# One value product for both parts of the attention weights, with changed scratch rings and later requests

## The chip, the cores and the metric

The kernel runs on one core of a Trainium2 chip. The metric is the device time of one execution in microseconds. Engines are named as in the profile: PE is TensorE, DVE VectorE, ACT ScalarE, POOL GpSimd, and SP the SyncE queue, from which most transfers are issued.

## What is computed

One layer of a bidirectional encoder on 1024 tokens (16 rows of 64) of width 1024, in float32. The reference, cut to the part in which the change lies:

```
h = h + 0.5 * swiglu(rms_norm(h, ffn1_norm), ...)
u = rms_norm(h, mix_norm);  z = u @ w_in
q, k, v, s_in, gates = split(z)
y_attn = neighbourhood_attention(q, k, v, na_rpb) @ w_attn_out   # 8 heads of 64, window 8 x 16
y_ssm  = s5_branch(s_in, ...) @ w_ssm_out                        # two scans, GELU, GLU
h = h + (sigmoid(g_attn) * y_attn + sigmoid(g_ssm) * y_ssm) @ w_out
h = h + 0.5 * swiglu(rms_norm(h, ffn2_norm), ...)
h = h + (p @ w_ple) * sigmoid(rms_norm(h, ple_norm) @ w_ple_gate)
out = rms_norm(h, final_norm)
```

In the attention, scores = q k / 8 + bias inside the window, a softmax, and the sum over the values v.

## The kernel before

**Precision in two parts.** The activations lie transposed, features on partitions and tokens along the free dimension, mostly as tiles of 128x512. A float32 operand is split into a high part (an ACT cast to fp32r) and a low part (a DVE subtraction); `split`, lines 152 to 154. A product is then three matmuls, high by high, high by low, low by high; `mm3`, lines 182 to 186.

**The order.** The order of TensorE's instructions is the program's (`manual_schedule` for PE, line 1801). For the other engines and the queues a planner with a time simulation orders them at build time (line 1800), except where a `manual_schedule` names DVE and ACT as well, as around `end()` (line 1723). Attention, scans and the GLU are written as a generator, `mixer_side` (line 1291). Projections call `tick()` after each three matmuls; when the count of a `yield n` has run down, the generator issues its next piece. So the attention units stand between pieces of the projections of q, k and the gates.

**Attention.** A unit is one head (8), one half of the rows (`rb`, 2) and one block of 16 columns (`cb`, 4): 64 units of 128 queries. Unit j issues `attn_scores` for itself (two matmuls; a DVE operation that adds the bias and finds the maximum; exponential, reciprocal and scaling), then `attn_turn` for unit j - 3, then `attn_values` for unit j - 5.

- `attn_turn` (line 1224) transposes three blocks of weights into one PSUM bank and splits them into `pth` (ACT) and `ptl` (DVE), two hid tiles of 128x384.
- `attn_values` (line 1235) does six matmuls. The values of a head lie side by side as high and low part, 64 columns each (`vhl`). With both as weights and `pth` as moving operand (128 columns), rows 0 to 63 of the bank O get high times high, rows 64 to 127 low times high (line 1240). With the high part alone as weights and `ptl` as moving operand, high times low is added to rows 0 to 63 (line 1242). One bank holds the four column blocks of a head half. After the fourth, ACT copies rows 64 to 127 out (line 1246), DVE adds the rest (line 1247), and the sum goes to `o_d`.
- `load_v` (line 1168) fetches values with four DMAs on SP into `vf` and splits them; `load_bias` (line 1181) fetches the bias rows of a head half into the single buffer `bt`, asked for in `make_tabs` right after the former ones were used.

From unit 48 on, `ssm_out` is added to each unit: two `emi` tiles are loaded by SP, and three units later six matmuls into the bank `yo` follow, whose copy goes to `y_d`. Lines 1356 to 1361 run the GLU after the last unit.

**Rings.** All 8 PSUM banks are one ring. In SBUF the tag `x` has 56 slots of 128x512: 32 for `u` (two halves, 8 tiles, high and low), the rest for hid tiles (`vhl`, the scores `sm`, `pth`, `ptl`, `emi`, the GLU's `yh`, `yl`, `wgh`, `wgl`) and later the operands of the branch products. In the middle stage the scratch kind `tmp` has a ring of its own with 4 buffers (line 1040): `vf`, `row`, `ot`, `ol`, `ys`, `gs`, `vs`, `sg`, `wgs`, `xn` and others. The kind `st`, for 128x1024 loads, has 3.

**Around it.** `gate_tile` (line 1365) computes one gate tile, copies it out of PSUM with ACT and stores it from SP to `g_d` at once. `load_br` (line 1405) loads the attention output of one half of the tokens from `o_d` for the branch products `br` (line 1490), two tiles of 128x1024, and splits them. `rstd` (line 204) is the reciprocal root of the norms: one ACT operation and three of DVE; `Norm.stat` (line 244) calls it. `end` (line 1683) writes out the order of the last steps.

Of the kernel before, what the change touches and what calls it, by code (L numbers as in the profile page):

```python
# [38 lines left out]
def encoder_block(ctx, tc, I, out):  # L39
# [50 lines left out]
    def dtile(name, shape):  # L90
        return dr.tile(list(shape), F32, name=name)
# [21 lines left out]
    a2_d = dtile("a2_d", [NF // 2, 7, P, HT])  # L113
    h2_d = dtile("h2_d", [P, NK * SEQ])
    v_d = dtile("v_d", [SEQ, 512])
    o_d = dtile("o_d", [512, SEQ])
    g_d = dtile("g_d", [16, P, SEQ])
    y_d = dtile("y_d", [NPD, P, NCH])
    y2_d = dtile("y2_d", [512, SEQ])
# [36 lines left out]
    def ksl(k):  # L156
        return slice(k * P, (k + 1) * P)
# [43 lines left out]

        return tc.issue_after(mark["ins"]) if "ins" in mark else nullcontext()

    def rstd(m, r, q):
        A.activation(r, m, AF.Abs_reciprocal_sqrt, bias=eps)
        V.tensor_tensor(q, r, r, ALU.mult)
        V.scalar_tensor_tensor(q, m, eps, q, ALU.add, ALU.mult)
        V.scalar_tensor_tensor(r, q, -3.0, r, ALU.add, ALU.mult)

    class Norm:  # L210
# [33 lines left out]
        def stat(self, r=None, summed=False):  # L244
            if summed:
                m = self.acc
            else:
                m = bank("ms")[:, 0:self.n]
                sums = [self.acc] + self.more
                for i, sq in enumerate(sums):  # L250
                    T.matmul(m, lhsT=ones, rhs=sq, start=i == 0, stop=i == len(sums) - 1)
            q = tmq("rq", [P, self.n])
            r = thid("rs", [P, self.n], F32) if r is None else r
            rstd(m, r, q)
            self.r = r

        def apply(self, gi, res, every):
# [779 lines left out]
    win = I["win"]  # L1037
    ap_cm = tc.tile_pool(name="ap", bufs=1, reuse_waits="tile")
    ap_ = ap_cm.__enter__()
    cur.update(st=(ap_, "st", 3), w=(ap_, "w", 12), tmp=(ap_, "tmp", 4))  # L1040

    def proj(w, t, name):
        o = bank(name)
# [123 lines left out]

    def load_v(hd, cb):
        n = 4 * KNC[cb]
        vf = tmp("vf", [P, 4, 64])  # L1170
        for g in range(4):
            nc.sync.dma_start(vf[0:n, g],
                              vdr[4 * g:4 * g + 4, KC0[cb]:KC0[cb] + KNC[cb], hd * 64:(hd + 1) * 64])
# [14 lines left out]
    def make_tabs(hd, rb):  # L1188
        b = 2 * hd + rb
        row = tmp("row", [P, 12, 32])  # L1190
        V.tensor_tensor(row, bts.pop(b),
                        rowm[:, rb].unsqueeze(2).broadcast_to([P, 12, 32]), ALU.add)
        load_bias(b + 1)
        res = []
        for v in range(3):
            n, f0 = (24, 32, 24)[v], (8, 0, 0)[v]
            tb = ap_.tile([P, 12, 32], F32, tag="tb", bufs=3, name="tb")
            V.tensor_tensor(tb[:, :, 0:n], row[:, :, f0:f0 + n],
                            colm[:, v, f0:f0 + n].unsqueeze(1).broadcast_to([P, 12, n]), ALU.add)
            res.append(tb)  # L1200
        tabs[hd, rb] = res
# [22 lines left out]
    def attn_turn(cb, sm):  # L1224
        kp = 4 * KNC[cb]
        tp = bank("pt")
        for g in range(3):
            T.transpose(tp[0:kp, ksl(g)], sm[:, g * kp:(g + 1) * kp], ident)
        ph = thid("pth", [P, 384])
        pl = thid("ptl", [P, 384])  # L1230
        A.copy(ph[0:kp], tp[0:kp, 0:384])
        V.tensor_tensor(pl[0:kp], tp[0:kp, 0:384], ph[0:kp].bitcast(F32), ALU.subtract)
        return ph, pl

    def attn_values(hd, rb, cb, O, ph, pl):
        kp = 4 * KNC[cb]
        hl = vld[hd, cb]
        for g in range(3):

            T.matmul(O[:, ksl(cb)], lhsT=hl[0:kp, rb + g].rearrange("p h d -> p (h d)"), rhs=ph[0:kp, ksl(g)], start=(g == 0), stop=False,  # L1240
                     skip_group_check=True)
            T.matmul(O[0:64, ksl(cb)], lhsT=hl[0:kp, rb + g, 0], rhs=pl[0:kp, ksl(g)], start=False, stop=(g == 2),
                     skip_group_check=True)
        if cb == 3:
            ot, ol = tmp("ot"), tmp("ol")
            A.copy(ol[0:64], O[64:128])
            V.tensor_tensor(ot[0:64].rearrange("p (r b c) -> p b r c", r=8, b=4),
                            O[0:64].rearrange("p (b r c) -> p b r c", b=4, r=8),
                            ol[0:64].rearrange("p (b r c) -> p b r c", b=4, r=8), ALU.add)
            nc.scalar.dma_start(o_d[hd * 64:(hd + 1) * 64, hsl(rb)], ot[0:64])  # L1250


    ydr = y_d.rearrange("g (t o) c -> g o t c", o=16)
# [37 lines left out]
    def mixer_side():  # L1291
        yield from u_second(14, 1)
        yield 8
        for r in range(2):
            V.memset(Xv[:, r, :, 0:1], 0.0)
            V.memset(Xv[:, r, :, XP - 1:XP], 0.0)
        ld = {}
        for pr in range(NPAIR):
            if pr in (0, 8):
                while pr // 4 not in stored:  # L1300
                    yield 1
                yield 8
                ld[pr] = inject_load(pr)
                yield 8
            if pr % 8 < 7:
                ld[pr + 1] = inject_load(pr + 1)
            inject(pr, *ld.pop(pr))
            yield 3
        while 0 not in qkv:
            scan_steps(1)  # L1310
            yield 1
        units = [(hd, rb, cb) for hd in range(NH) for rb in range(2) for cb in range(4)]
        n = len(units)
        for cb in range(4):
            load_v(0, cb)
        load_bias(0)
        make_tabs(0, 0)
        scan_steps(4)
        yield 6
        sms, pts, O = {}, {}, {}  # L1320
        so = {}
        SO = 48
        for j in range(n + 6):
            if j < n:
                hd, rb, cb = units[j]
                while hd not in qkv:
                    yield 1
                if cb == 0 and j > 0:
                    make_tabs(hd, rb)
                sms[j] = attn_scores(hd, rb, cb)  # L1330
            if 0 <= j - 3 < n:
                pts[j - 3] = attn_turn(units[j - 3][2], sms.pop(j - 3))
            if 0 <= j - 5 < n:
                hd, rb, cb = units[j - 5]
                if cb == 0:
                    O[hd, rb] = bank("O")
                attn_values(hd, rb, cb, O[hd, rb], *pts.pop(j - 5))
                if rb == 1 and hd + 1 < NH:
                    load_v(hd + 1, cb)
# [12 lines left out]
        yield 4  # L1352
        for m in range(4):
            glu_load(m)
        yield 13
        for t in range(2):
            glu_split(t)
            yield 4
            for m in range(4):
                glu_out(m, t)  # L1360
                yield 4

    start(mixer_side())

    def gate_tile(w, m, t):
        o = proj(w, t, "gt")
        gs = tmp("gs")
        A.copy(gs, o)
        nc.sync.dma_start(g_d[m, :, hsl(t)], gs)


    for m0 in range(0, 4, 2):
# [32 lines left out]
    def load_br(t, b):  # L1405

        res = []
        if b == 0:
            for k in range(0, 4, 2):
                st = tst("br")  # L1410
                nc.sync.dma_start(st.rearrange("p (k c) -> p k c", k=2),
                                  o_d[k * P:(k + 2) * P, hsl(t)].rearrange("(k p) c -> p k c", p=P))
                for i in range(2):
                    hi, lo = tx("bh"), tx("bl")
                    split(hi, lo, st[:, hsl(i)])
                    res.append((hi, lo))
            return res
        for k in range(4):
# [33 lines left out]
    W = [loadw(win[16 + m]) for m in (14, 15)]  # L1452
    for i in range(2):
        gate_tile(W[i], 14 + i, 0)
    drain()
    oy = [[load_br(0, 0)], []]
    W0 = [load_was(0)]
# [1 line left out]
    oy[0].append(load_br(0, 1))  # L1459
    for i in range(2):  # L1460
        gate_tile(W[i], 14 + i, 1)
    for b in range(2):
        oy[1].append(load_br(1, b))

# [218 lines left out]
    def end():  # L1683
# [131 lines left out]
```

## Time and profile before

| | |
|---|---|
| three runs | 2103.85, 2105.74, 2106.14 us; median 2105.74 |
| profiled execution: its time, its span | 2107.16 us, 2105.4 us |
| granted clock of TensorE, mean | 0.998 |
| HBM read, written | 201.01 MB, 82.31 MB |
| attention units | first scores at 838.5 us, last values at 1108.9 us |
| copies to `o_d`, and the branch products' first matmul | last at 1113.8 us; 1172.3 us |

How to read the rows: a group shows line, engine, operation, out<-in by the program's names, the shapes, the count, and then busy time, mean duration and the engine's idle time ahead of it with what ended it. A wait row shows who waited for whom, and then the total in us, the number of waits and the longest. A timeline row has its start in us from the span's start, its duration and, in brackets, the idle time before it. A tile row shows the shortest, median and longest duration in ns, first and last start, and the forms. A window row shows the length and then busy time and instruction count of PE, PEld (weight loads), DVE, ACT and POOL, the granted clock, the DMA engines' busy share and GB/s. Matmuls overlap: the next one starts while the one before it still drains, so the distance from start to start tells what one costs, not its duration.

### The profile page before, as it was taken

How to read it: one execution, taken by the hardware profiler on the slowest of the kernel's cores; microseconds unless marked ns; L12 is line 12 of the kernel's file. 1: busy time of each engine (PE TensorE's matmuls, PEld its weight loads, DVE VectorE, ACT ScalarE, POOL GpSimd, SP SyncE). 2: the span in 40 equal slices, each digit the busy share in tenths (PEclk: the TensorE clock that was granted, in tenths of full speed). 3: DMA queues.
4: the chain of work that ended last, by engine and by line, in shares of the span. 5: the costliest groups of instructions: out<-in, count | busy, mean ns of one | idle time of the engine just before them, and what ended most of it. 6: DMA issues, size and time to landing. Idle time of an engine off the chain costs nothing.

```text
span 2105.4 us, 28053 instructions
## 1 busy us (share of the span) xinstructions
PE 2078.4 (99%) x9662; PEld 1706.3 (81%) x9662; DVE 1417.4 (67%) x2420; ACT 1000.4 (48%) x1832; POOL 399.9 (19%) x636
## 2 busy tenths in 40 slices
PE   8999999999999999999999999899999999999998
PEld 3788888888888888888888888688888888888886
DVE  7897776667967334677653668886566665786855
ACT  6434333434445333666774635543333334445543
POOL 0037555541000006888200011000000000000000
PEclk9999999999999999999999999999999999999999
DMA  3435344475543552233467754143323238533302
GB/s 133 143 118 153 126 135 126 140 267 167 185 120 106 168 176 68 64 97 98 126 201 261 255 171 93 53 157 112 110 85 126 90 113 295 159 109 91 120 21 81
DMA packets 197744, 285.19 MB, mean 135 GB/s; under 512 B 41568, under 2 KB 81120, under 8 KB 197600
## 3 DMA queue, kind: packets, MB, share of 16 engines
q1 hardware_dynamic: 180304, 258.20, 38.9%
q10 hardware_dynamic: 14992, 21.00, 2.9%
q0 software_dynamic: 2304, 4.20, 1.3%
q8 instruction: 76, 1.25, 0.2%
q14 instruction: 68, 0.56, 0.1%
HBM read 201.01 MB, written 82.31 MB: 135 GB/s over the span
## 4 chain that ended last, share of the span: by engine, by line
PE 91%; DVE 4%; DMA 2%; ACT 2%; issue 1%; SPq 0%; DVEq 0%; ACTq 0%
PE dx L184 4%; PE dx L186 4%; PE dx L185 4%; PE ux L184 3%; PE ux L185 3%; PE gx L184 3%; PE ux L186 3%; PE gx L185 3%; PE gx L186 3%; PE gt L184 3%; PE gt L185 3%; PE gt L186 3%; PE dy L184 2%; PE dy L185 2%; PE dy L186 2%; PE uy L184 2%
## 5 line engine op out<-in xcount | busy, mean ns | idle before, releaser
L153 ACT CAST wh<-hbuf 128x512 fp32r<-128x512 f32 x280 | 172.9, 622 | 389.8 <-PE gx L185 80.9
L154 DVE TENSOR_TENSOR wl<-hbuf,wh 128x512 fp32r<-128x512 f32 x280 | 210.7, 755 | 124.6 <-ACT wh L153 122.3
L153 ACT CAST wh<-wblk 128x512 fp32r<-128x512 f32 x190 | 117.9, 622 | 187.0 <-PE dx L185 80.6
L184 PE MATMUL dx<-ah,wh 128*128 128x512 f32 x416 | 164.4, 395 | 3.2 <-DVE hbuf L1559 2.9
L154 DVE TENSOR_TENSOR wl<-wblk,wh 128x512 fp32r<-128x512 f32 x190 | 130.3, 689 | 52.7 <-ACT wh L153 47.3
L186 PE MATMUL dx<-ah,wl 128*128 128x512 f32 x416 | 162.6, 391 | 0.0
L185 PE MATMUL dx<-al,wh 128*128 128x512 f32 x416 | 162.4, 390 | 0.0
L154 DVE TENSOR_TENSOR al<-araw,ah 128x512 fp32r<-128x512 f32 x154 | 106.0, 692 | 51.9 <-PE dx L185 21.1
L1097 POOL TENSOR_TENSOR sc<-X,rho 128x128 f32<-128x128 f32 x128 | 76.8, 600 | 329.0 <-ACT X L1080 319.1
L184 PE MATMUL gx<-xh,wh 128*128 128x512 f32 x320 | 125.1, 391 | 1.2 <-DVE c L580 1.2
L184 PE MATMUL ux<-xh,wh 128*128 128x512 f32 x320 | 125.1, 391 | 0.4 <-DVE c L580 0.4
L186 PE MATMUL gx<-xh,wl 128*128 128x512 f32 x320 | 124.5, 389 | 0.0
L186 PE MATMUL ux<-xh,wl 128*128 128x512 f32 x320 | 124.5, 389 | 0.0
L185 PE MATMUL gx<-xl,wh 128*128 128x512 f32 x320 | 124.5, 389 | 0.0
L185 PE MATMUL ux<-xl,wh 128*128 128x512 f32 x320 | 124.5, 389 | 0.0
L153 ACT CAST ah<-araw 128x512 fp32r<-128x512 f32 x154 | 95.0, 619 | 46.0 <-PE dx L185 12.7
L184 PE MATMUL gt<-xh,wh 128*128 128x512 f32 x256 | 102.7, 401 | 0.0
L186 PE MATMUL gt<-xh,wl 128*128 128x512 f32 x256 | 99.8, 390 | 0.0
L185 PE MATMUL gt<-xl,wh 128*128 128x512 f32 x256 | 99.8, 390 | 0.0
L184 PEld LDWEIGHTS dx<-ah,wh 128*128 128x128 f32 x416 | 78.5, 189 | 22.0 <-DVE hbuf L1559 3.9
L185 PEld LDWEIGHTS dx<-al,wh 128*128 128x128 f32 x416 | 78.5, 189 | 16.8 <-issue 0.7
L186 PEld LDWEIGHTS dx<-ah,wl 128*128 128x128 f32 x416 | 78.4, 189 | 16.6
(381 smaller groups left out, 5605.2 us busy)
## 6 DMA issues: line engine op xcount, KB each, us to landing
araw<-a_d SPq DMA_DIRECT2D x154, 256.0 KB
a_d<-c SPq DMA_DIRECT2D x148, 256.0 KB
wblk<-in_wd SPq DMA_DIRECT2D x88, 256.0 KB
hbuf<-in_wg SPq DMA_DIRECT2D x40, 512.0 KB
hbuf<-in_wu SPq DMA_DIRECT2D x40, 512.0 KB
wst<-in_win SPq DMA_DIRECT2D x26, 512.0 KB
hbuf<-in_xT SPq DMA_DIRECT2D x32, 256.0 KB
h_d<-hbuf ACTq DMA_DIRECT2D x32, 256.0 KB
```

Source lines behind the costliest of these rows:

```text
L153: A.copy(hi, src)
L154: return eng.tensor_tensor(lo, src, hi.bitcast(F32), ALU.subtract)
L184: T.matmul(o, lhsT=wh, rhs=xh, start=first, stop=False, skip_group_check=more)
L185: T.matmul(o, lhsT=wh, rhs=xl, start=False, stop=False, skip_group_check=more)
L186: T.matmul(o, lhsT=wl, rhs=xh, start=False, stop=last, skip_group_check=more)
L1097: G.tensor_tensor(sc, both, rho4, ALU.mult)
```

## The change

- `attn_turn` writes both parts of the transposed weights into one tile `ptb` (three blocks, each with 128 high and 128 low columns) in a ring of two in the middle stage's pool; `attn_values` does one product of 256 columns for each block. A bank O holds two column blocks, with the products of the high and of the low weights beside each other.
- After each second block, ACT copies rows 64 to 127 (low values by high weights) and rows 0 to 63 (high by high) of the bank's high columns, and DVE adds rows 0 to 63 of its low columns. The two sums are stored as two planes of `o_d`; `load_br` loads both planes and adds them with DVE. Low values by low weights are computed too and not used.
- In a unit, `attn_values` (and `load_v`) is issued ahead of `attn_turn`.
- The kind `tmp` of the middle stage is taken from the ring `x`; `vf` has two buffers of its own.
- The bias rows are asked for at the third column block of a head half, in place of directly after the use of the former ones.
- A gate's store is issued after the copy of the next gate tile; `store_gate()` without arguments issues the one that is held.
- `rstd` and `stat` take a function `mid`, called after the ACT operation; in `end` the scalings of the tiles 6 and 7 move there.

```
-    o_d = dtile("o_d", [512, SEQ])
+    o_d = dtile("o_d", [2, 512, SEQ])
...
-    def rstd(m, r, q):
+    def rstd(m, r, q, mid=None):
         A.activation(r, m, AF.Abs_reciprocal_sqrt, bias=eps)
+        if mid is not None:
+            mid()
         V.tensor_tensor(q, r, r, ALU.mult)
...
-    cur.update(st=(ap_, "st", 3), w=(ap_, "w", 12), tmp=(ap_, "tmp", 4))
+    cur.update(st=(ap_, "st", 3), w=(ap_, "w", 12), tmp=(sb, "x", NX))
...
-        vf = tmp("vf", [P, 4, 64])
+        vf = ap_.tile([P, 4, 64], F32, tag="vf", bufs=2, name="vf")
...
                         rowm[:, rb].unsqueeze(2).broadcast_to([P, 12, 32]), ALU.add)
-        load_bias(b + 1)
...
-        ph = thid("pth", [P, 384])
-        pl = thid("ptl", [P, 384])
-        A.copy(ph[0:kp], tp[0:kp, 0:384])
-        V.tensor_tensor(pl[0:kp], tp[0:kp, 0:384], ph[0:kp].bitcast(F32), ALU.subtract)
-        return ph, pl
+        pb = ap_.tile([P, 3, 2, P], F32R, tag="ptb", bufs=2, name="ptb")
+        src = tp[0:kp, 0:384].rearrange("p (g q) -> p g q", g=3)
+        A.copy(pb[0:kp, :, 0], src)
+        V.tensor_tensor(pb[0:kp, :, 1], src, pb[0:kp, :, 0].bitcast(F32), ALU.subtract)
+        return pb
...
+        o = O["o"][:, (cb % 2) * 256:(cb % 2) * 256 + 256]
         for g in range(3):
-            T.matmul(O[:, ksl(cb)], lhsT=hl[0:kp, rb + g].rearrange("p h d -> p (h d)"), rhs=ph[0:kp, ksl(g)], start=(g == 0), stop=False,
+            T.matmul(o, lhsT=hl[0:kp, rb + g].rearrange("p h d -> p (h d)"), rhs=pb[0:kp, g].rearrange("p h q -> p (h q)"), start=(g == 0), stop=(g == 2),
                      skip_group_check=True)
-            T.matmul(O[0:64, ksl(cb)], lhsT=hl[0:kp, rb + g, 0], rhs=pl[0:kp, ksl(g)], start=False, stop=(g == 2),
-                     skip_group_check=True)
+        if cb % 2 == 0:
+            return
+        if cb == 1:
+            O["t"] = tmp("ot")
+        ov = O["t"].rearrange("p (r b c) -> p b r c", r=8, b=4)[:, cb - 1:cb + 1]
+        src = O["o"].rearrange("p (b h r c) -> p h b r c", b=2, h=2, r=8)
+        A.copy(ov[64:128], src[64:128, 0])
+        A.copy(ov[0:64], src[0:64, 0])
+        V.tensor_tensor(ov[0:64], src[0:64, 1], ov[0:64], ALU.add)
         if cb == 3:
...
-            nc.scalar.dma_start(o_d[hd * 64:(hd + 1) * 64, hsl(rb)], ot[0:64])
+            nc.scalar.dma_start(o_d[:, hd * 64:(hd + 1) * 64, hsl(rb)], O["t"])
...
+                if cb == 2:
+                    load_bias(2 * hd + rb + 1)
                 sms[j] = attn_scores(hd, rb, cb)
+            if 0 <= j - 5 < n:
+                hd, rb, cb = units[j - 5]
+                if cb % 2 == 0:
+                    O.setdefault((hd, rb), {})["o"] = bank("O")
+                attn_values(hd, rb, cb, O[hd, rb], pts.pop(j - 5))
+                if rb == 1 and hd + 1 < NH:
+                    load_v(hd + 1, cb)
             if 0 <= j - 3 < n:
                 pts[j - 3] = attn_turn(units[j - 3][2], sms.pop(j - 3))
-            if 0 <= j - 5 < n:
...
+    held = []
+    def store_gate(*new):
+        for gs, m, t in held:
+            nc.sync.dma_start(g_d[m, :, hsl(t)], gs)
+        held[:] = [new] if new else []
...
         A.copy(gs, o)
-        nc.sync.dma_start(g_d[m, :, hsl(t)], gs)
+        store_gate(gs, m, t)
...
-                st = tst("br")
-                nc.sync.dma_start(st.rearrange("p (k c) -> p k c", k=2),
-                                  o_d[k * P:(k + 2) * P, hsl(t)].rearrange("(k p) c -> p k c", p=P))
+                st = [tst("br") for _ in range(2)]
+                for w in range(2):
+                    nc.sync.dma_start(st[w].rearrange("p (k c) -> p k c", k=2),
+                                      o_d[w, k * P:(k + 2) * P, hsl(t)].rearrange("(k p) c -> p k c", p=P))
+                V.tensor_tensor(st[0], st[0], st[1], ALU.add)
...
-        scaled(6, six[3])
         added(a, b, s, hm)
         fin[2].square(7, V)
-        scaled(7, hm)
         finish(1, (4, 6))
-        fin[2].stat()
+        fin[2].stat(mid=lambda: (scaled(6, six[3]), scaled(7, hm)))
         finish(2)
```

More of the change, by code (lines that the diff above doesn't have):

```diff
@@ L242, in bring, with stat @@
             self.rest = sq
-        def stat(self, r=None, summed=False):
+        def stat(self, r=None, summed=False, mid=None):
             if summed:
@@ L253, in stat @@
             r = thid("rs", [P, self.n], F32) if r is None else r
-            rstd(m, r, q)
+            rstd(m, r, q, mid)
             self.r = r
@@ L1228, in attn_turn, with attn_values @@
             T.transpose(tp[0:kp, ksl(g)], sm[:, g * kp:(g + 1) * kp], ident)
-        ph = thid("pth", [P, 384])
-        pl = thid("ptl", [P, 384])
-        A.copy(ph[0:kp], tp[0:kp, 0:384])
-        V.tensor_tensor(pl[0:kp], tp[0:kp, 0:384], ph[0:kp].bitcast(F32), ALU.subtract)
-        return ph, pl
-    def attn_values(hd, rb, cb, O, ph, pl):
+        pb = ap_.tile([P, 3, 2, P], F32R, tag="ptb", bufs=2, name="ptb")
[3 more added lines that the diff above has]
+        return pb
+    def attn_values(hd, rb, cb, O, pb):
         kp = 4 * KNC[cb]
         hl = vld[hd, cb]
+        o = O["o"][:, (cb % 2) * 256:(cb % 2) * 256 + 256]
         for g in range(3):
-            T.matmul(O[:, ksl(cb)], lhsT=hl[0:kp, rb + g].rearrange("p h d -> p (h d)"), rhs=ph[0:kp, ksl(g)], start=(g == 0), stop=False,
+            T.matmul(o, lhsT=hl[0:kp, rb + g].rearrange("p h d -> p (h d)"), rhs=pb[0:kp, g].rearrange("p h q -> p (h q)"), start=(g == 0), stop=(g == 2),
                      skip_group_check=True)
-            T.matmul(O[0:64, ksl(cb)], lhsT=hl[0:kp, rb + g, 0], rhs=pl[0:kp, ksl(g)], start=False, stop=(g == 2),
-                     skip_group_check=True)
-        if cb == 3:
[L1245 to L1249, printed above, removed]
-            nc.scalar.dma_start(o_d[hd * 64:(hd + 1) * 64, hsl(rb)], ot[0:64])
+        if cb % 2 == 0:
[7 more added lines that the diff above has]
+        V.tensor_tensor(ov[0:64], src[0:64, 1], ov[0:64], ALU.add)
+        if cb == 3:
+            nc.scalar.dma_start(o_d[:, hd * 64:(hd + 1) * 64, hsl(rb)], O["t"])
     ydr = y_d.rearrange("g (t o) c -> g o t c", o=16)
@@ L1329, in mixer_side @@
                     make_tabs(hd, rb)
+                if cb == 2:
+                    load_bias(2 * hd + rb + 1)
                 sms[j] = attn_scores(hd, rb, cb)
+            if 0 <= j - 5 < n:
[5 more added lines that the diff above has]
+                    load_v(hd + 1, cb)
             if 0 <= j - 3 < n:
                 pts[j - 3] = attn_turn(units[j - 3][2], sms.pop(j - 3))
-            if 0 <= j - 5 < n:
[L1334 to L1339, printed above, removed]
             scan_steps(2)
@@ L1409, in load_br @@
             for k in range(0, 4, 2):
-                st = tst("br")
-                nc.sync.dma_start(st.rearrange("p (k c) -> p k c", k=2),
-                                  o_d[k * P:(k + 2) * P, hsl(t)].rearrange("(k p) c -> p k c", p=P))
+                st = [tst("br") for _ in range(2)]
[3 more added lines that the diff above has]
+                V.tensor_tensor(st[0], st[0], st[1], ALU.add)
                 for i in range(2):
                     hi, lo = tx("bh"), tx("bl")
-                    split(hi, lo, st[:, hsl(i)])
+                    split(hi, lo, st[0][:, hsl(i)])
                     res.append((hi, lo))
@@ L1454, in encoder_block @@
         gate_tile(W[i], 14 + i, 0)
+    store_gate()
     drain()
@@ L1461, in encoder_block @@
         gate_tile(W[i], 14 + i, 1)
+    store_gate()
     for b in range(2):
```

## The prediction

> **What bounds the kernel now.** I read the page first: engine shares, then the chain that ended last.
>
> ```profile
> span 2105.4 us, 28053 instructions
> PE 2078.4 (99%) x9662; PEld 1706.3 (81%) x9662; DVE 1417.4 (67%) x2420; ACT 1000.4 (48%) x1832; POOL 399.9 (19%) x636
> ...
> PE 91%; DVE 4%; DMA 2%; ACT 2%; issue 1%; SPq 0%; DVEq 0%; ACTq 0%
> ...
> L153 ACT CAST wh<-hbuf 128x512 fp32r<-128x512 f32 x280 | 172.9, 622 | 389.8 <-PE gx L185 80.9
> L154 DVE TENSOR_TENSOR wl<-hbuf,wh 128x512 fp32r<-128x512 f32 x280 | 210.7, 755 | 124.6 <-ACT wh L153 122.3
> ```
>
> TensorE is busy for 2078.4 of 2105.4 us and carries 91% of the last chain. So an edit is worth what it takes from TensorE's issue, plus the waits of TensorE that it removes or makes. Next I asked what TensorE waits for:
>
> ```profile
> PE g L656 <- ACT xg L336: 4.9, 1, 4.9
> ...
> PE yo L1122 <- DVE ot L1247: 1.5, 1, 1.5
> ...
> PE yo L1122 <- DMA emi<-u_d: 0.7, 1, 0.7
> ```
>
> Columns: total us, times, longest. The largest, at 4.9 us, is at the start of the kernel. The two rows of yo lie in the attention stage, and no row of the answer names the loads of vf, the bias rows or the gate stores. All parts of the change but the tail and the later addition of two planes sit in that stage, so most of its edits to queues and rings can only matter by what they add.
>
> Busy time hides how matmuls follow each other, as they overlap. What counts is the distance from start to start. I therefore read TensorE's timeline for one whole attention unit (columns: start, duration):
>
> ```profile
> 936.40 0.49 PE L1228 MATMUL pt<-ident,sm 128*96 128x128 f32 x3
> 936.65 0.31 PE L1240 MATMUL O<-pth,vhl 128*128 128x128 f32 x1
> 936.79 0.22 PE L1242 MATMUL O<-ptl,vhl 128*64 128x128 f32 x1
> 936.85 0.27 PE L1240 MATMUL O<-pth,vhl 128*128 128x128 f32 x1
> 936.96 0.22 PE L1242 MATMUL O<-ptl,vhl 128*64 128x128 f32 x1
> ...
> 937.48 0.40 PE L185 MATMUL q<-xl,wh 128*128 128x512 f32 x1
> ```
>
> From the product with pth (128 wide weights) to the one with ptl (64 wide) it takes 0.11 us, at the first of the unit 0.14; from there to the next pth product 0.06. One pair is thus 0.17 us, though each product streams only 128 columns. From the first transpose at 936.40 to the second projection matmul at 937.48 there are 1.08 us.
>
> **The value product.** The change puts pth and ptl side by side and makes one product of 256 columns with the full 128 wide weights: three matmuls a unit in place of six. They are also issued ahead of the transposes, straight after the scores. Two rows give the price. The end of the kernel has products with 128x128 weights and 256 columns of the same type:
>
> ```profile
> 2085.20 0.28 PE L184 MATMUL pg<-xh,whh 128*128 128x256 f32 x1
> 2085.32 0.28 PE L185 MATMUL pg<-xl,whh 128*128 128x256 f32 x1
> ```
>
> They follow each other every 0.12 us. And one early unit had no values yet, so that its transposes stand directly ahead of a projection, as they will in every unit after the change:
>
> ```profile
> 851.03 0.29 PE L1212 MATMUL s<-kh,qs 128*128 128x288 f32 x1
> 851.16 0.30 PE L1213 MATMUL s<-kl,qs 128*128 128x288 f32 x1
> 851.30 0.49 PE L1228 MATMUL pt<-ident,sm 128*128 128x128 f32 x3
> ...
> 851.86 0.39 PE L185 MATMUL gt<-xl,wh 128*128 128x512 f32 x1
> 852.09 0.39 PE L186 MATMUL gt<-xh,wl 128*128 128x512 f32 x1
> ```
>
> A projection matmul that follows its like takes 0.23 us (851.86 to 852.09). Before: 1.08 - 0.23 = 0.85 us a unit for transposes and values. After: the transposes up to the second projection matmul 0.56 (851.30 to 851.86) less 0.23, so 0.33, and three value products at 0.12, together 0.69. That saves 0.16 us a unit.
>
> ```profile
> L1240 PE MATMUL O<-pth,vhl x192: 220/276/306, 855.0 to 1108.8; 96*128 96x128 f32 x96, 128*128 128x128 f32 x96
> L1242 PE MATMUL O<-ptl,vhl x192: 221/223/263, 855.1 to 1108.9; 96*64 96x128 f32 x96, 128*64 128x128 f32 x96
> L1246 ACT COPY ol<-O x16: 582/584/587, 867.9 to 1112.4; 64x512 f32<-64x512 f32 x16
> L1247 DVE TENSOR_TENSOR ot<-O,ol x16: 673/683/684, 868.5 to 1113.1; 64x512 f32<-64x512 f32 x16
> ```
>
> With 192 / 3 = 64 units the term is 64 x 0.16 = 10.2 us. The bounds of the new product: 0.11, the 128 column product with full weights, gives 0.19 a unit and 12.2 us; 0.13, the 288 column score product (851.03 to 851.16), gives 0.13 and 8.3 us. I take 0.12, which is the row of the very shape.
>
> [...]
>
> **Reading out the values.** Before, each of 16 head halves took one ACT copy of 0.58 and one DVE addition of 0.68. After, it takes four ACT copies and two DVE additions of 64x256, and the third summand travels to memory in a plane of its own. The rows of that size:
>
> ```profile
> L1080 ACT COPY X<-inj x32: 358/368/372, 742.5 to 801.2; 64x256 f32<-64x256 f32 x32
> L1082 DVE COPY X<-inj x32: 417/424/429, 742.9 to 800.7; 64x256 f32<-64x256 f32 x32
> ```
>
> ACT gains 16 x (4 x 0.37 - 0.58) = 14.4 us of work, DVE 16 x (2 x 0.42 - 0.68) = 2.6 us, spread over the 250 us from 855 to 1109. Casts and subtractions of pth and ptl keep their sizes. The cover is ACT's idle time in that stage:
>
> ```profile
> 1050.00:1100.00 50.00, 49.35 (x348) 44.82 (x348) 29.04 (x83) 37.16 (x92) 0.00 (x0) 1.00 0.72 205
> 1100.00:1150.00 50.00, 50.00 (x240) 41.78 (x239) 18.21 (x27) 26.43 (x43) 0.00 (x0) 1.00 0.77 259
> ```
>
> In its fullest 50 us ACT (the fourth busy column) works for 37.2; 2.9 more of copies make 40, and shorter units some 83% of the time. I cost it at nothing on TensorE; were ACT full there, the 14.4 us would come back whole.
>
> **Scratch tiles in the large ring.** All tmp tiles leave their ring of four and share the 56 slots with u (32) and the hid tiles; pth and ptl leave it. What the ring of four cost shows here:
>
> ```profile
> 1038.99 0.56 DVE L1191 TENSOR_TENSOR row<-bt,rowm 128x384 f32<-128x384 f32 x1 [2.12 <-DMA y_d<-ys]
> ...
> 1042.34 0.68 DVE L1247 TENSOR_TENSOR ot<-O,ol 64x512 f32<-64x512 f32 x1
> ```
>
> VectorE stood 2.12 us for a scratch slot that a store still held, came late to ot, and TensorE waited its 1.5 us for that bank. With the larger ring this goes: 1.5 us. Late next are the emi loads (the 0.7 us wait), which I leave as it is. By the code the slots wanted at once in the last sixteen units are 8 vhl, 5 sm, 6 pth and ptl, 8 emi before, 27 for 24; after, up to 6 scratch tiles replace the 6.
>
> **Queues.** SyncE's own waits:
>
> ```profile
> SPq L1369 <- ACT gs L1368: 43.8, 25, 6.6
> SPq L1186 <- DVE row L1191: 29.3, 10, 7.2
> SPq L1172 <- DVE stat L1220: 16.7, 6, 5.0
> ```
>
> Gate stores issued one tile later and bias rows asked for two units later should lose most of the first two. Nothing follows, as TensorE waited for no load behind them; the bias row still has two units before its use. The vf loads get two buffers of their own: a load now waits for the VectorE subtraction two loads back, and behind it on SyncE stand the emi loads, weights and bias rows. Bounds from the rows of yo: a gain of 0.7 up to a loss of 0.7 in each of 16 state products; I take zero, since no TensorE wait names vf now.
>
> **Joining the planes, and the tail.** Four more loads of 512 KB and four additions of 128x1024 (about 1.5 us each, twice the 0.755 of a 128x512 subtraction):
>
> ```profile
> L184 PE MATMUL br<-bh,wh x32: 389/389/389, 1172.3 to 1193.3; 128*128 128x512 f32 x32
> ...
> L1411 SPq DMA_DIRECT2D br<-o_d x4: 370/373/385, 1122.1 to 1149.1; - x4
> ```
>
> The last old load is issued 23 us ahead of the first product. From 1100 to 1150 the DMA engines are 0.77 busy and VectorE 18 of 50 us, so two loads and two additions a half fit; cost nothing, and without the cover 6 us of additions. At the very end two ACT scalings move behind the root:
>
> ```profile
> 2095.46 0.70 PE L251 MATMUL ms<-sq,ones 128*128 128x256 f32 x2 [0.70 <-DVE sq L232]
> ...
> 2096.23 0.45 ACT L205 ACTIVATE rs<-ms,eps 128x256 f32<-128x256 f32 x1
> ```
>
> The root needs the sum that ends at 2096.16 and starts at 2096.23: at most 0.07 us to gain, and the scalings then run under three VectorE steps. I count zero.
>
> **The sum.** -10.2 for the products, -1.5 for the slot wait, +1.0 for one new wait of the size of those two of yo, since every ACT and DVE order in the stage is planned anew: -10.7 us. The profiled execution took 2107.16 us (span 2105.4) and would take 2096.5; it lies 1.4 above the median of 2105.74, which becomes 2095.0.
>
> **The rivals.** Part of it is given back (12%). In the GLU the 24 slots besides u hold 16 halves of y and 8 of weights exactly; scratch tiles now want some of them, so two late pairs in the GLU and two in the branch loads are split only when slots come free, each 0.62 + 0.76 us in sight of TensorE: 5.5 us, 2100.5. For it: that arithmetic. Against: products of other work lie between, and no such wait shows.
>
> Streaming alone sets the cost (7%): were a pair worth two of its shorter gap, 2 x 0.06 = 0.12, the new product would save nothing, and only the 1.5 us would remain: 2104.2. Against it is the 0.11 in every pair. [...]
>
> Slower (9%): the two vf buffers hold SyncE, the emi loads behind them come late, and each of 16 state products in the last units waits 1.0 us, between the 0.7 and 1.5 seen: +16, 2111. It decides from 14.9 / 16 = 0.93 us each. For it: one emi load is late already. Against: a buffer is wanted again only two units later, and vf is loaded in half of the units.
>
> The change does not do what it says (2%): the new product needs the same slots as the pair, 2105.7.
>
> **How the numbers follow.** About 0.2%, 4.2 us, is what a measurement of this kernel can tell from no change. My case has 70%: its own range runs from 12.2 + 2.2 of gain with no new wait, 2091.3, to 8.3 with no wait removed and 3 of new ones, 2100.4. The range reaches on to the part given back, 2103, and 1.3 below. Faster: 70 and 10 of the 12 points; same: 2 + 7 + 2; slower 9.
>
> **What would show it.** Right: value products 0.12 apart, transposes directly ahead of a projection, units shorter by 0.16, no wait of yo for ot, other stages as long as before. Wrong: gaps of 0.17 a product; new TensorE waits for emi, yh, bh or an O bank that sum to over 5 us; ACT over 90% in the last units.

## The result, and the profile after

The change makes the kernel slower: 2154.91 us (median of 5 runs, 2152.97 to 2157.02) beside 2105.74 us before; the ratio is 1.0236, with a 95% interval of 1.0222 to 1.025. The prediction was 2095.0 us and faster. The page of the changed kernel, in the lines that were shown of the one before:

```profile
span 2155.2 us, 27784 instructions
PE 2093.4 (97%) x9470; PEld 1709.8 (79%) x9470; DVE 1423.0 (66%) x2440; ACT 1007.5 (47%) x1880; POOL 400.3 (19%) x636
...
PE 42%; DMA 5%; DVE 2%; ACT 1%; SPq 1%; issue 1%; ACTq 0%; DVEq 0%
```

TensorE has 192 matmuls fewer, as planned, and yet 15 us more of busy time. So matmuls ran slower, and there are waits besides. No engine became the bound: ACT and DVE are as busy as before. What TensorE waits for, in the changed kernel (total us, times, longest):

```profile
PE br L184 <- ACT bh L153: 12.7, 3, 5.6
PE O L1243 <- DVE ptb L1233: 9.6, 4, 7.8
PE glu L185 <- DVE yl L154: 7.2, 1, 7.2
...
PE gt L184 <- DVE ot L1254: 2.7, 1, 2.7
...
PE pt L1229 <- ACT gs L1385: 2.0, 1, 2.0
PE inj L1075 <- DMA ut<-u_d: 1.9, 2, 1.6
```

Such waits the prediction had named as the sign that it would be wrong. To see when the time is lost, I set the starts of TensorE's stages in the two traces side by side (us from the span's start):

| | before | after | difference |
|---|---|---|---|
| first gate tile after u's second half | 718.99 | 725.03 | +6.0 |
| a projection of q, in the attention | 922.39 | 927.29 | +4.9 |
| a projection of k, still in the attention | 1000.12 | 1003.06 | +2.9 |
| first branch product | 1172.25 | 1205.41 | +33.2 |
| the products after the branches | 1259.29 | 1312.43 | +53.1 |

So 6 us go ahead of the attention, the early attention gains, and some 50 are lost from the last units to the branches. Three places in the trace of the changed kernel show how. The first is u's second half, on DVE:

```profile
710.96 0.74 DVE L264 SCALAR_TENSOR_TENSOR xn<-hbuf,gains,rs 128x512 f32<-128x512 f32 x1
712.39 0.69 DVE L154 TENSOR_TENSOR xl<-xn,xh 128x512 fp32r<-128x512 f32 x1 [0.68 <-ACT xh L153]
713.00 0.74 DVE L264 SCALAR_TENSOR_TENSOR xn<-hbuf,gains,rs 128x512 f32<-128x512 f32 x1
```

One xn, its cast on ACT, its subtraction, and only then the next xn: 2.04 us a tile. The scratch tile xn now comes from the large ring, and by this row it gets one slot there. Before, four xn were made in a row.

The second is a store. The attention output of a head half goes out as one DMA over both planes. This is the first of them, as the DMA view of a window of 6.5 us; the digits are the busy tenths of all 16 engines in 40 slices, the other line gives packets, MB and share of the 16 engines of the ACT queue:

```profile
DMA  1110010130012001111111111122222222212223
...
q10 hardware_dynamic: 130, 0.26, 12.5%
```

and the one of the kernel before, in a window of 2 us:

```profile
DMA  0019759849659774332111110110000000000000
...
q10 hardware_dynamic: 80, 0.13, 26.3%
```

Before, 64 packets of 2048 B and 16 small ones go over in 1.2 us, with up to nine tenths of the 16 engines busy. After, 128 packets and 2 small ones take the whole 6.5 us, and 12.5% of 16 engines is the time of 2 engines. In the late units other transfers wait for this store. SP's waits for it in the changed kernel (total us, times, longest; 41.7 us in all, beside 7.7 before) are those of the loads of emi, hbuf and yt:

```profile
SPq L1110 <- DMA o_d<-ot: 24.8, 4, 9.1
SPq L1493 <- DMA o_d<-ot: 10.1, 1, 10.1
SPq L1266 <- DMA o_d<-ot: 6.8, 1, 6.8
```

ACT and then SP, at the time of the store of 1070.4 to 1077.0 us:

```profile
1072.90 0.82 ACT L1118 COPY xs<-X 64x256 f32<-64x256 f32 x2
1077.00 0.37 ACTq L1129 DMA_DIRECT2D y_d<-ys  x1
1077.41 0.61 ACT L1222 ACTIVATE sm<-sm,stat 128x384 f32<-128x384 f32 x1 [3.69 <-DMA vf<-v_d]
```

```profile
1071.55 0.69 SPq L1109 DMA_DIRECT2D emi<-e_d  x1
1077.41 0.32 SPq L1110 DMA_DIRECT2D emi<-u_d  x1
```

ACT stands with a small store in its queue, SP with a load, until the large store is over; the softmax steps and readouts behind it on ACT stand too. (In the next such store ACT's small one is issued 2.6 us before the end, SP's load again only after it.) The third place is what TensorE does after such a wait:

```profile
1120.93 0.39 PE L185 MATMUL gt<-xl,wh 128*128 128x512 f32 x1
1121.16 0.39 PE L186 MATMUL gt<-xh,wl 128*128 128x512 f32 x1
1129.39 1.01 PE L1243 MATMUL O<-ptb,vhl 96*128 96x256 f32 x3 [7.84 <-DVE ptb L1233]
1130.20 0.63 PE L184 MATMUL gt<-xh,wh 128*128 128x512 f32 x1
1130.63 0.63 PE L185 MATMUL gt<-xl,wh 128*128 128x512 f32 x1
```

The projections follow each other every 0.43 us instead of 0.23. The granted clock (third column from the end) of the changed kernel is, in a window of 50 us and in the part of it around this wait:

```profile
1100.00:1150.00 50.00, 41.04 (x200) 34.76 (x200) 12.67 (x22) 26.37 (x50) 0.00 (x0) 0.86 0.62 181
```

```profile
1123.90:1134.10 10.20, 4.71 (x13) 3.84 (x14) 2.67 (x5) 4.60 (x10) 0.00 (x0) 0.50 0.80 213
```

while before it was 1.00 in the first of them. So clock is lost beside the wait of 7.84 us: it is 0.50 from 1123.9, within the wait, to 1134.1 us. The gain that was planned is there as well:

```profile
937.12 0.52 PE L1243 MATMUL O<-ptb,vhl 96*128 96x256 f32 x3
937.47 0.49 PE L1229 MATMUL pt<-ident,sm 128*128 128x128 f32 x3
...
938.03 0.39 PE L185 MATMUL q<-xl,wh 128*128 128x512 f32 x1
```

Three value products take 0.35 us up to the transposes. Undisturbed units come every 3.71 and 3.80 us, before every 3.84 and 3.93.

### The profile page after: what moved, and what is told of

The parts are those of the page before. It is cut to its first block, busy times and chain, and to the rows that moved or that the text cites. A ratio compares the mean times of both kernels' runs of the same rounds, so it can differ in the third digit from the quotient of the medians.

```text
span 2155.2 us, 27784 instructions
## 1 busy us (share of the span) xinstructions
PE 2093.4 (97%) x9470; PEld 1709.8 (79%) x9470; DVE 1423.0 (66%) x2440; ACT 1007.5 (47%) x1880; POOL 400.3 (19%) x636
## 4 chain that ended last, share of the span: by engine, by line
PE 42%; DMA 5%; DVE 2%; ACT 1%; SPq 1%; issue 1%; ACTq 0%; DVEq 0%
PE dx L184 2%; PE dx L185 2%; PE dx L186 2%; PE ux L184 2%; PE gx L184 2%; PE gx L185 2%; PE ux L185 2%; PE ux L186 2%; PE gx L186 2%; PE dy L185 1%; PE dy L184 1%; PE dy L186 1%; PE br L185 1%; PE br L186 1%; DMA o_d<-ot 1%; PE pg L186 1%
## 5 line engine op out<-in xcount | busy, mean ns | idle before, releaser
L424 DVE TENSOR_TENSOR hbuf<-hbuf 128x512 f32<-128x512 f32 x120 | 90.4, 754 | 2.6 <-DMA hbuf<-in_wu 0.5
```

Source lines behind the costliest of these rows:

```text
L424: V.tensor_tensor(b11, (b12, b22, None, None, b21)[i - 2], b11, ALU.subtract)
```

## The experiments

Each run is given by its median and, where it matters, its ratio to the kernel before with the 95% interval. Stage shifts compare profiled executions.

**First four: one part of the change alone, or all but one.** My theories were A, the scratch tiles in the large ring, and B, the second plane.

e1: the kernel before with the wide product, the values ahead of the transposes, one plane, all rings and requests old. As the ring of two for ptb has no room, the weights' splits are two hid tiles, pta and ptc.

```
+  pa, pc = thid("pta", [P, 2, 2, P]), thid("ptc", [P, 1, 2, P])
+  T.matmul(o, lhsT=hl(128 columns), rhs=pb[g] (256 columns), ...)   # 3 in place of 6
+  one plane: ov = src[64:128, 0] + src[0:64, 0] + src[0:64, 1]
```

> The kernel before with the wide value product alone: both parts of the weights in two hid tiles (two casts and two subtractions a unit in place of one each), values ahead of the transposes, the three summands of a head half added on the chip into one plane of o_d; scratch ring, vf, bias rows and gate stores as before. Theory A (the loss comes from the scratch tiles in the ring x, the product itself pays about 10 us): 2094 to 2098 us. Theory B (the second plane, with its loads and additions queued ahead of other work, loses the time): also 2094 to 2098, as there is one plane here. If the product itself or the smaller share of an O bank loses: over 2110.

Measured: 2115.1 us, 1.0046 (1.0031 to 1.0061). Both theories missed; the third case, a loss over 2110, came. Its waits of TensorE:

```profile
PE O L1245 <- DVE ptc L1234: 7.7, 8, 2.0
PE O L1245 <- DVE pta L1234: 5.5, 4, 1.9
```

The splits stand late in DVE's order, behind steps of 1.3 us and more (at 895.12 us one of 1.39 stands ahead of a split for which TensorE waits 1.95), and cost more than the product gains.

e2: the rings alone, the old pair of products; the values are ahead of the transposes here too.

```
-  tmp=(ap_, "tmp", 4)
+  tmp=(sb, "x", NX);  vf, pth, ptl: two buffers each in the stage's pool
```

> The kernel before with the rings of the change alone: scratch tiles from the ring x, vf with two buffers, pth and ptl in two buffers each in the room that becomes free, values ahead of the transposes for that; products of 128 columns, one plane, requests as before. Theory A: 2140 to 2165 us, with TensorE waits at the end of the second half of u, in the GLU and in the branch products. Theory B: 2100 to 2115.

Measured: 2132.73 us, 1.0128 (1.011 to 1.0147), between the two ranges. The rings alone cost 28 us: +5 at u's second half and +19 at the branches, where the wait is

```profile
PE br L184 <- ACT bh L153: 11.4, 3, 7.2
```

The GLU and the late units lose nothing, so A is one cause and not the whole.

e3: the whole change with the old ring of four scratch tiles.

```
-  tmp=(sb, "x", NX)
+  tmp=(ap_, "tmp", 4);  vf = tmp("vf", ...);  pta, ptc as in e1
```

> The changed kernel with the rings of before: scratch ring of four, vf in it, both parts of the weights in two hid tiles; the wide product, two planes, later bias rows and gate stores and the tail as in the change. Theory A: 2095 to 2103 us. Theory B: 2120 to 2145, with the waits of the GLU and of the branch products still there.

Measured: 2166.34 us, 1.0292 (1.0276 to 1.0307), above both ranges and the slowest of all:

```profile
PE O L1246 <- DVE pta L1235: 38.0, 10, 7.4
PE O L1246 <- DVE ptc L1235: 10.4, 10, 2.0
```

The loss lies in the attention, none in the branches. A ring was thus not all of it, and why this ring was so bad stayed open until e17.

e4: the later requests alone, for bias rows and gate stores.

> The kernel before with the bias rows asked for two units later and the gate stores one gate tile later, nothing else. Theories A and B alike: 2104 to 2107 us, no change that can be measured. If the held gate stores (a scratch slot of four kept longer) matter: 2110 or more.

Measured: 2101.63 us, 0.9984 (0.9975 to 0.9993). I had put this at nothing; it gains 3.3 us. Most of it are waits of TensorE: yo waits 0.6 us for ot instead of 1.5 and no longer for emi (0.7 before), v 0.7 us for its weights instead of 1.8.

**The cost of a pair.** e5 changes one line of the kernel before: the product with ptl takes all 128 weight columns.

```
-  T.matmul(O[0:64, ksl(cb)], lhsT=hl[0:kp, rb + g, 0], rhs=pl...)
+  T.matmul(O[:, ksl(cb)], lhsT=hl[0:kp, rb + g] (h d), rhs=pl...)
```

> The kernel before with one line changed: the product with ptl takes all 128 columns of the value weights and writes all 128 partitions of O, as the product with pth does (so vlo times ptl is added as well). Nothing is moved, no ring, request or readout is touched. Theory W (the 0.17 us of a pair come from the turn between 128 and 64 weight columns: 0.11 us to the narrow product, 0.06 back): two equal products of 128 columns take 0.06 us each, 0.12 a pair as the 256-column product does, and 64 units x 3 x 0.05 = 10 us go: 2093 to 2098. Theory S (a new set of weights costs 0.11 us however it is shaped, and the narrow one is the cheap one): pairs of 0.17 to 0.22 us, 2105 to 2115.

Measured: 2113.89 us, 1.0044 (1.0031 to 1.0057), theory S. TensorE's timeline:

```profile
938.27 0.27 PE L1242 MATMUL O<-ptl,vhl 128*128 128x128 f32 x1
938.38 0.27 PE L1240 MATMUL O<-pth,vhl 128*128 128x128 f32 x1
938.49 0.27 PE L1242 MATMUL O<-ptl,vhl 128*128 128x128 f32 x1
```

Each product of 128 columns now takes 0.11 us, although it streams no more than the 0.06 us one did. What costs here is the new set of weights, by its columns, 0.06 us for 64 and 0.11 for 128: in the kernel before, the load of a 64 wide set starts at 936.73, the next one, 128 wide, at 936.79, and the one after it at 936.90. 256 moving columns ride along for 0.12.

**Taking the causes out one by one.** e7 is the changed kernel with one plane: both parts are added at the readout, as in e1, and the branch loads are the old ones.

> The changed kernel, but the two halves of a pair of units' values are added at the readout into one plane of 64 rows, as before; branch loads are the old ones, one load and no addition. Scratch tiles stay in the x ring, the wide product, the ring for values and the later requests stay. Theory B (the second plane: its loads and its two additions queued ahead of yl and bh): the 7.2 us wait of GLU for yl goes and the gt wait for ot (2.7 us) as well, the branch waits of 12.7 us fall below 6: 2125 to 2138. Theory A (x slots taken by scratch): u's second half (+6) and the branch loads (+25 or more) stay, 2140 to 2152.

Measured: 2119.2 us, 35.7 less than the change. The waits for ptb and yl are gone; those at br (10.7 us) and the +5.9 at u's second half stay. It came out faster than both ranges: the plane costs more than I had thought, and the ring still costs.

e8 is e7 with the scratch tiles in a ring of three beside the ring of two for vf, and pta and ptc as in e1.

> The changed kernel with one plane, and with the scratch tiles out of the x ring: a ring of three scratch tiles and the ring of two for values' loads stand in the room that the ring of four scratch tiles had; pt's splits are two tiles of the old hid ring. Wide product and later requests stay. Theory A (x slots): u's second half loses 1 to 3 us (three xn tiles for four), branch loads nothing: 2092 to 2104. Theory C (pt's splits stand late in DVE's and ACT's order whatever the rings are): TensorE waits for pta and ptc of 8 us or more in all, and 2105 to 2125.

Measured: 2105.75 us, 1.0006 (0.9997 to 1.0015). All stage losses are gone but for

```profile
PE O L1246 <- DVE ptc L1235: 8.9, 6, 2.5
```

which is theory C: without ptb's own ring the splits come late.

e9 is the changed kernel with only xn and the later br loads taken out of the large ring; they use ptb's two buffers, idle at both times.

```
-  xn = tmq("xn")
+  xn = at("xn", [P, 768], F32, "xn")[:, 0:HT]     # ring "ptb", two buffers
-  st = tmp("br")
+  st = at("xn", [P, 768], F32, "br")[:, 0:HT]
```

> The changed kernel with nothing but two kinds of scratch tile taken out of the x ring: xn of u's second half and br of the later branch loads take their room in the ring of two that ptb has, which is idle at both times. Theory A (x slots are what these two places lack): the +6 us at the projection after u's second half fall to 0 to 3, the branch waits for bh of 12.7 us to under 4: 2115 to 2135. Theory B (the second plane) leaves them: 2148 to 2155, with branch waits for bh over 8 us.

Measured: 2132.33 us, 22.6 less than the change, as A said for these places. The +6 becomes -0.8, the wait at br 1.7. What is left are B's waits:

```profile
PE O L1243 <- DVE ptb L1233: 10.3, 3, 7.8
PE glu L185 <- DVE yl L154: 5.8, 1, 5.8
```

e10 has both repairs, e7's and e9's.

> The changed kernel with both repairs at once: the values of a pair of units are added into one plane at the readout, and xn of u's second half and br of the later branch loads have their room apart from the x ring. Theory of two causes (the exhausted x ring at two places, and the second plane; each repair alone gave 22.6 and 35.7 us, together 58.3 of 2154.9): 2094 to 2099, which is where the prediction stood, with no TensorE wait over 2 us from 700 to 1280 us. Theory of one queue (a late unit anywhere drags the others; the two repairs overlap): 2104 to 2115. Theory S (the product itself does not gain so much): 2100 to 2106, with no waits.

Measured: 2094.8 us, 0.995 (0.9937 to 0.9962). It beats both kernels, as the theory of two causes had it. The largest wait left from the attention to the branches is one of 0.4 us, of br for bh.

**What in the second plane costs.** e11 and e12 split it. e11 keeps the readout and the store of two planes and loads only the first; e12 is e10 with the loads and additions put back.

```
 e11:  st = tst("br");  load o_d[0, ...];  no addition
 e12:  st = [tst("br"), tst("br")];  both from the one plane;  V.tensor_tensor(st[0], st[0], st[1], ALU.max)
```

> The changed kernel with xn and br apart, and with both planes written at the readout and stored as in the change; the branch loads fetch the first plane alone, as one load, and add nothing (the second plane's part of the values is left out). If the loads and additions of the second plane are what costs (one load and one addition more for each pair of tiles, in a ring of three): 2094 to 2102. If the readout and the stores of 128 rows are: 2120 to 2132, with the waits of O for ptb near 7 us and of glu for yl left.

> The kernel with both repairs, and with the branch's loads and additions of the change put back: the one plane is loaded into two tiles, whose maximum is then taken in the addition's place. If the loads and additions cost: 2120 to 2132, glu waiting 5 us or more for yl. If the readout and the stores did: 2094 to 2102.

Measured: 2125.89 us and 2098.47 us. Beside e10, loads and additions cost some 4 us (e12's runs lie between 2095.3 and 2103.7), readout and store 31. In e11's waits the one for ptb is as long as in the change, though nothing is loaded twice; that for yl, which I expected to stay, is no longer among the largest. It is gone in e12 too (0.6 us), which has the additions, so it takes both, the addition's place on DVE and the store.

e14 and e15 cut the store in two, on the change itself and on e9.

```
-  nc.scalar.dma_start(o_d[:, hd * 64:(hd + 1) * 64, hsl(rb)], O["t"])
+  for w in range(2):
+      nc.scalar.dma_start(o_d[w, hd * 64:(hd + 1) * 64, hsl(rb)], O["t"][w * 64:(w + 1) * 64])
```

> The changed kernel with one statement altered: the 128 rows of a pair of units are stored by two DMAs, one for each plane of 64 rows, instead of one DMA over both planes. Theory D (one store over two planes runs on about two DMA engines, 128 packets of 84 ns in 6 to 9 us, and what shares its engines and its place in the queues waits): each store takes 0.7 to 2 us, the waits of O for ptb and of glu for yl go, and of the 49 us some 28 come back: 2119 to 2128, the waits at br and the +6 of u's second half staying. Theory E (the readout's extra ACT copy, or the 128 KB more, is what holds ACT and DVE): 2148 to 2157.

> The same two stores, and xn of u's second half and br of the later branch loads with room apart from the x ring; both planes are kept, loaded and added as in the change. Theory D: 2097 to 2103, the one-plane kernel's 2094.8 and 4 for the second plane's loads and additions, which one run measured. Theory E: 2122 to 2134.

Measured: 2120.96 us and 2098.13 us (0.9968, 0.9957 to 0.9978), both as theory D has it. One statement brings 34 us. The first two stores of e14, in a window of 2 us:

```profile
DMA  0000319569539339141108556915935963110000
...
q10 hardware_dynamic: 160, 0.26, 57.5%
```

The same 128 packets, with 32 small ones, are through in 1.5 us. SP's waits for these stores sum to 2.9 us instead of 41.7.

e16 makes the opposite test: e10, whose store has 64 rows, with a destination in two halves.

```
-  o_d[hd * 64:(hd + 1) * 64, hsl(rb)]
+  o_d[hd * 64:(hd + 1) * 64, hsl(rb)].rearrange("(i w) c -> w i c", w=2)
```

> The kernel with both repairs and one plane (2094.8 us), but each store's 64 rows go to every second row of their place, first half and then second half, by one DMA with a destination of two halves; the same bytes, and the value columns of a head come out in another order. Theory D: the 64 packets go over about two engines and spread over 3 us or more instead of 0.7 to 2, and the time rises by 3 to 20 us: 2098 to 2115. Theory E: 2093 to 2097.

Measured: 2107.92 us, 13.1 more than e10. The same bytes in the same 64 packets take 3.6 to 6.2 us (in e10 0.8 to 2.1), on some 12% of 16 engines:

```profile
DMA  1113100000400101111111111111011111110000
...
q10 hardware_dynamic: 65, 0.13, 11.9%
```

So the shape of the destination does it, not the readout and not the bytes.

e17 is e3 with its store cut in two.

> The third kernel (the change with the old ring of four scratch tiles, vf in it, pt's splits in two hid tiles) with its store cut into one for each plane. Theory D (the store on two engines holds its scratch tile and all that is queued behind it): of the 61 us lost some 40 or more come back, waits for pta under 15 us, 2112 to 2128. Theory F (the ring of four itself is too small once vf, ot over two units and a held gate tile share it): over 2145, with waits for pta of 25 us and more.

Measured: 2114.24 us, 52 less than e3:

```profile
PE O L1246 <- DVE pta L1235: 6.3, 4, 3.1
PE O L1246 <- DVE ptc L1235: 5.5, 8, 1.6
```

So it was not the ring's size that cost most of the 38 us; the slow store held its tile. SP, whose vf tiles come from the same ring, waited 68.4 us for the store ahead of these loads in e3, and 13.8 us here.

**The product by itself.** e13 is e10 with the 128 and the 64 wide products put back.

```
-  T.matmul(o, lhsT=hl (h d), rhs=pb[g] (h q), ...)
+  T.matmul(o[:, 0:P], lhsT=hl (h d), rhs=pb[g, 0], ...)
+  T.matmul(o[0:64, 0:P], lhsT=hl[..., 0], rhs=pb[g, 1], ...)
```

> The kernel with both repairs, but with each unit's values made as before by pairs of a 128-wide and a 64-wide product on the two halves of ptb, and one addition less in the readout; everything else as there. Theory W: 64 units x 3 x 0.05 to 0.06 us: 9 to 11 us more than with the wide product, and no TensorE waits. Theory S (the wide product gains nothing once its cover is kept): within 3 us of it.

Measured: 2109.83 us, 15.0 more than e10, and 12.7 by the profiled spans: more than either theory said. Units come every 3.92 and 3.82 us against 3.79 and 3.69, so 64 x 0.13 = 8.3 us are the matmuls'. 2.5 us are waits for ptb, which theory W did not expect; the rest, 2 to 4 us, I did not trace.

## Why the prediction was wrong, point by point

- **The value product** was right in kind: 0.12 us a product, transposes directly ahead of a projection. The term was 0.16 us a unit; measured 0.13, the lower bound, which came from the score product: 8.3 us for 10.2. The rival "streaming alone sets the cost" is out, by e5 and e13. In the traces a pair of a 128 and a 64 wide set takes 0.17 us, one of two 128 wide sets (e5) 0.22 to 0.23.
- **"The third summand travels to memory in a plane of its own."** This is the step that failed first. I costed the copies that make the plane and the loads that fetch it, and gave the store between them no line at all; I took it to be a store like the old one with twice the rows. It ran for 6.1 to 9.0 us. e14 (34 us back by one statement), e16 (13 us lost by its counterpart) and e17 show it. The destination's slowest dimension became the planes, 2, and the first of these stores, in a window of 6.5 us, had 2 small packets and 12.5% of 16 DMA engines, the time of 2; a store of 64 rows had 16 small ones, and 26.3% of a window of 2 us. How the share follows from the shape, no run shows. I had read the diff line with `o_d[:, ...]` and not asked what it does to the pattern.
- **"Scratch tiles in the large ring."** This is the second step that failed. The 1.5 us of the slot wait are gone in e10 (in the change itself TensorE waits for ot at other places, 2.7 and 0.5 us). But I counted slots in the last sixteen units and the GLU alone. The ring also serves u's second half, where xn had four tiles and now gets one, and the branch loads, where br waits for its slot. e9 prices the two places at 22.6 us. The rival "part of it is given back" had the right mechanism, at 5.5 us, and half of it in the wrong place, the GLU, whose wait came from the store and the addition.
- **"Late next are the emi loads", +1.0 for new waits.** The waits sum to over 35 us. They follow from the two causes above, since e10 has next to none of them. The rival of the slower side, the two vf buffers, was not it: e10 and e15 keep that ring and lose nothing there.
- **Queues, at zero.** The later requests gain 3.3 us (e4). I had reasoned that TensorE waits for no load behind them. But most of the gain is in waits that the list did name, for emi, for ot and for v's weights, and that I left as they were or gave to the ring.
- **Joining the planes, at zero.** With the store repaired, e12 prices it at 4 us. In the change itself it is part of the 7.2 us wait for yl: the addition stood ahead of yl on DVE and waited for a load, `[8.56 <-DMA hbuf<-h_d]` in the timeline, while SP in turn waited 10.1 us for a store to `o_d` ahead of an hbuf load. I had counted DVE's idle time, not its order.
- **The readout on ACT, at nothing**, held: e15 has those copies and takes 2098.13 us. The tail was not tried apart.
- **2094.8 us for e10 beside 2095.0 predicted** is in part chance. e10 is not the change: it has another readout and keeps two kinds of tile out of the large ring, and it has the later requests, which I had at zero and which alone gained 3.3 us.

The two causes add up. The store costs 34.0 us with the ring's two places as in the change (e14) and 34.2 with them repaired (e15 beside e9); the two places cost 22.6 and 22.8. Without both, the changed kernel takes 2098.1 us (e15), and one plane saves the last 3.

The traces also part the waits from the clock. By the pages TensorE's idle time rose from 27.0 to 61.8 us, so 34.8 are waits. Its busy time rose by 15.0, though the product takes 8.3 less, so slower matmuls cost some 23. Between 700 and 1260 us the granted clock is 0.50 in eight stretches, with TensorE busy for 38.3 us; half of that, 19 us, is an estimate of what the slow clock cost. Some 4 us are left open.

## What to carry to other kernels

For each DMA whose shape a change touches, look at the slowest dimension of its destination, and at its own packets in the profile: here a store to a view of 2 by 64 rows took 6.1 to 9.0 us, and two stores of 64 (the first pair of e14) together 1.5. When scratch tiles move to a shared ring, count its slots in every stage that takes tiles from it, not in the stage that the change is about. A planned gain on TensorE is worth nothing where a cast on the way to it stands on its engine behind an issue that waits, as the steps on ACT did here for 3.3 us.

## What the runs showed of the hardware

- A store of 128 rows of 2048 B took 6.1 to 9.0 us as 2 x 64; as two stores of 64 rows (e14), each took 0.7 to 2.4 us, the first pair together 1.5. While it ran, loads on SP waited for it, 41.7 us in all, and a small store on ACT 3.3 us (1073.7 to 1077.0 us). The 12.5% in the first 6.5 us are the time of 2 engines of 16; no run here tells engines apart.
- After the wait of 7.84 us, matmuls of 512 columns followed each other every 0.43 us instead of 0.23 for 4.7 us. The eight stretches at a granted clock of 0.50 last from 3.4 to 13.7 us. Why the clock comes down, no run shows. The trace has 0.50 also without a long wait ahead of it: at u's second half TensorE was busy for 1.97 of the 3.4 us from 710.9 us, with no wait over 0.6 us, and then the clock was 0.50 from 714.3 to 721.1 us. So 6.0 us are lost there, though TensorE stood idle for only 1.7.
- A product with 128 weight columns costs 0.11 us with 128 moving columns (e5) and 0.12 with 256 (the changed kernel), and with 64 weight columns 0.06 (the kernel before, 128 moving columns).
